# Staging the first two 512-token chunks as wholes, from tiles at the other end of SBUF

## The chip, the core and the metric

The kernel runs on one core of a Trainium2 chip. A time is the device time of one execution in microseconds (us); several executions give a median. The profiled execution is a single one, with a span (from its first instruction to its last) and a time of its own.

## What is computed

Two transformer blocks over 2048 tokens of 1024 features. Only the head of the first block matters here:

```python
mod = c_act @ w_ada + b_ada                       # 6 x 1024 numbers, from the conditioning vector c
sh1, sc1, ... = split(mod, 6)
h = rmsnorm(x, ln1_pre) * (1 + sc1) + sh1         # x: 2048 x 1024
proj = h @ w_in                                   # 22 groups of 128 columns
# then sliding-window attention over 6 of the groups, a gated recurrence over 16,
# an output projection, a mixture of experts, and a second block
```

Each matrix product is made from three products of float32r parts: every operand is split into a rounded part (`hi`) and what is left (`lo`), and `hi*lo + hi*hi + lo*hi` is summed in PSUM.

## The kernel before, in words

All generators of a stage ("lanes") are run by a scheduler, `B.run`, when the program is built. It keeps a planned clock for each engine and its own costs of operations, and lets a lane emit its next instruction when the planned clock says that its inputs are ready. So the order of the instructions on each engine is fixed by the plan, and the chip then runs each engine in that order. `Pool.get` and `B.bank` hand out buffers and wait until one is free; `B.bank("pA")` gives one of two PSUM banks of that tag, and there are four tags (`pA`, `pS`, `pU`, `pT`) of two banks, eight banks in all. Nearly every instruction is recorded at line 122, that of the helper which issues it, so the rows are told apart by their tiles.

The first stage is `P1.run`. Its lanes, around the change:

- `mod_first` loads 16 tiles of `wadaT` (128x1024 float32, 512 KB each, tiles `mh` and `ml`), seven ahead, and takes a dot product of each with the activated vector `cact` on VectorE (`mod_dot`). At the tenth it sets the flag `x`; after the sixteenth `first()` makes the scales `a1` and shifts `sh1` of the norm and sets the flag `mod`.
- `h_lane` waits for `x` and then goes over the 4 chunks of 512 tokens and the 4 tiles of 128 tokens in each: it loads a tile of `x` into one of two buffers `xl` and spawns `h_block`. That squares and sums it on ScalarE (output `jk`), takes the inverse root on VectorE (`rsqrt`, 13 small operations on tiles `xrv`, `xry`, `xrt`), scales the tile by it on GpSimd (`xl<-xl,xry`), waits for `mod`, transposes the tile in two halves of four 128x128 blocks into a bank `pT`, and gives `xl` back. For each half `h_part` evicts the four blocks with scale and shift into `hf` (one half on VectorE, one on ScalarE), rounds them on ScalarE into `hhi`, and subtracts on VectorE into `hlo`. When all eight halves of a chunk are done, `self.h[c]` is set.
- `h_tiles` gives the `hhi` and `hlo` of a chunk; there are two sets, so chunks 2 and 3 wait until chunks 0 and 1 have been used for the first half of the sequence.
- `W.lane` waits for `x`, loads the groups of `w_in`, rounds them on GpSimd (`whi`), subtracts on VectorE (`wlo`), and stores both to DRAM (`WIN`) for the second half. Four groups are held.
- `lane_a` projects: for each group, both chunks of a half (`proj`, which waits for `self.h[c]`, then 24 matmuls of 128x512 in a bank `pA`). The first group is the keys: `ev_k` evicts them into `KH` and `KL` with four ScalarE and four VectorE instructions, after the flag `("swa", half)`; the second is the values, then the queries.
- `swa(half)` opens the attention's tiles (`KH`, `KL`, `VS`, `ndist`) and runs the attention units; `hgrn` the recurrence; `mod_rest` the other 32 tiles of `wadaT`, once chunk 1 is staged.

Of the kernel before, what the change touches and what calls it, by code (L numbers as in the profile page):

```python
# [10 lines left out]
F32 = mybir.dt.float32  # L11
F32R = mybir.dt.float32r
BF16 = mybir.dt.bfloat16
# [3 lines left out]
AF = mybir.ActivationFunctionType  # L17
OP = mybir.AluOpType
# [5 lines left out]
D = 1024  # L24
KT = 8
# [3 lines left out]
BLOCK = None  # L29
# [149 lines left out]
class Pool:  # L179
    def __init__(self, pool, clock):  # L180
        self.pool, self.clock, self.rings, self.slots = pool, clock, {}, {}
# [26 lines left out]
class B:  # L208
# [15 lines left out]
        nc.vector.memset(self.eps, EPS)  # L224

    @contextmanager
    def pool(self, name):
        with self.tc.tile_pool(name=name, bufs=2, reuse_waits="tile") as p:
            yield Pool(p, self.clock)

    def phase(self, name):
# [86 lines left out]
    def run(self, *lanes, back=(), first=()):  # L318


        lanes, first = list(lanes), list(first)
        back = list(back) + [g for g in self.lanes if g not in first]
        c = self.clock
        idle = 0
        while lanes or self.spawned:
            state = BLOCK
            for g in first + self.spawned + lanes + back:
                try:
                    r = next(g)
                except StopIteration:  # L330
                    for l in (first, self.spawned, lanes, back, self.lanes):
                        if g in l:
                            l.remove(g)
                    state = 1
                    break
                if r:
                    state = r
                    break
                if r is not BLOCK:
                    state = 0  # L340
            if state:
                idle = 0
                continue
            c.now += 0.05
            idle = idle + 1 if state is BLOCK else 0
            if idle >= 400:
                assert False, "every lane is blocked"
# [28 lines left out]
            (lambda: V.scalar_tensor_tensor(out, t, 1.5, y, op0=OP.add, op1=OP.mult), (t,)))  # L376
        return out

    def rsqrt(self, ss, n, scale, name, out=None):

        V = self.nc.vector
        v, y, t = (self.small([128, n], name + z) for z in "vyt")
        out = y if out is None else out
        yi = y.bitcast(I32)
        newton = [(lambda: V.tensor_tensor(t, y, y, op=OP.mult), (y,)),
                  (lambda: V.tensor_tensor(t, t, v, op=OP.mult), (t,)),
                  (lambda: V.scalar_tensor_tensor(y, t, 1.5, y, op0=OP.add, op1=OP.mult), (t,))]
        yield from self.steps("vector",
            (lambda: V.tensor_scalar(v, ss, scale, EPS, op0=OP.mult, op1=OP.add), (ss,)),
            (lambda: V.tensor_scalar(yi, v.bitcast(I32), 1, None, op0=OP.logical_shift_right), (v,)),  # L390
            (lambda: V.tensor_scalar(yi, yi, -1.0, float(0x5F3759DF), op0=OP.mult, op1=OP.add), (y,)),
            (lambda: V.tensor_scalar(v, v, -0.5, None, op0=OP.mult), (v,)),
            *newton, *newton, *newton[:2],
            (lambda: V.scalar_tensor_tensor(out, t, 1.5, y, op0=OP.add, op1=OP.mult), (t,)))
        return out


class Weights:
# [4 lines left out]
    def __init__(self, b, ld, pool, srcs, ring, shape=(128, 1024), ahead=2, lo="vector", store=None, keep=None):  # L403
        self.b, self.ld, self.pool, self.srcs, self.ring, self.shape, self.ahead = b, ld, pool, srcs, ring, list(shape), ahead
        self.store, self.keep = store, keep or {}
        self.hl, self.eng, self.hi_eng = {}, lo, "gpsimd"
        self.extra, self.taken = None, 0
        self.writing = set()
# [105 lines left out]
def pipe(units, depth):  # L514


    live, more = [], True
    it = iter(units)
    while live or more:
        state = BLOCK  # L520
        if more and len(live) < depth:
            try:
                u = next(it)
                if u is not BLOCK:
                    live.append(u)
            except StopIteration:
                more = False
        for u in list(live):
            try:
                c = next(u)  # L530
            except StopIteration:
                state = 1
                live.remove(u)
                break
            if c:
                state = c
                break
            if c is not BLOCK:
                state = 0
        if live or more:  # L540
            yield state
# [9 lines left out]
class P1:  # L551
# [41 lines left out]
    def mod_first(self):  # L593

        b, I = self.b, self.I
        ws, n = [], 0
        for j in range(16):
            while n < min(16, j + 7):
                w = yield from self.Wp.get([128, D], F32, "m" + "hl"[n % 2], tag=("whi", "wlo")[n % 2], bufs=4)
                yield from b.load(w, I["wadaT"][n])  # L600
                ws.append(w)
                n += 1
            w = ws.pop(0)
            yield from self.mod_dot(j, w)
            b.done(w)
            if j == 9:
                self.flags.add("x")
        self.nc.vector.tensor_tensor(self.mod1, self.mod1, b.bada[:, 0:16], op=OP.add)
        self.first()
        self.flags.add("mod")  # L610
        yield 1
# [32 lines left out]
        nc.vector.tensor_scalar(self.hw, b.vec[:, HON, 0:4], 0.5, None, op0=OP.mult)  # L644


    def h_lane(self):

        b = self.b
        yield from self.wait("x")  # L650
        for c in range(4):
            for t in range(4):
                x = yield from self.ld.get([128, D], F32, "xl", bufs=self.nxl)
                r = (c * 4 + t) * 128
                yield from b.load(x, self.I["x"][r:r + 128, :])
                b.spawn(self.h_block(c, x, slice(t * 128, t * 128 + 128)))
# [405 lines left out]

    def swa(self, half):
        b, nc, I = self.b, self.nc, self.I
        with b.pool("p1a") as P:
            self.P = P
            self.la, self.lb, self.po = Lock(), Lock(), {}
            self.KH = P.tile([128, 2, 1152], F32R, name="KH", bufs=1)
            self.KL = P.tile([128, 2, 1152], F32R, name="KL", bufs=1)
            self.VS = P.tile([128, 9, 2, 2, 64], F32R, name="VS", bufs=1)  # L1070
            self.ndist = P.tile([128, 256], F32, name="ndist", bufs=1)
            nc.sync.dma_start(self.ndist, I["ndist"])
            new = [self.KH[:, :, 0:128], self.KL[:, :, 0:128], self.VS[:, 0]]
            old = [self.KH[:, :, 1024:], self.KL[:, :, 1024:], self.VS[:, 8]]
            if half:
                for a, o in zip(self.carry, new):
                    nc.gpsimd.tensor_copy(o, a.bitcast(F32))
            self.flags.add(("swa", half))
            yield from pipe(self.swa_units(half), 7)
            if half == 0:  # L1080
                for a, o in zip(self.carry, old):
                    nc.gpsimd.tensor_copy(a, o.bitcast(F32))
# [19 lines left out]
    def run(self):  # L1102
        b, tc, nc, I = self.b, self.b.tc, self.nc, self.I
        st, en = b.phase("p1")
        with st:
            b.nld, self.nxl, self.nmd = 2, 2, 1
            self.ld, self.Sp, self.X, self.POp = en("ld"), en("p1s"), en("p1x"), en("p1po")
            self.carry = [self.Sp.tile(s, F32R, name=f"c{i}", bufs=1) for i, s in enumerate(([128, 2, 128], [128, 2, 128], [128, 2, 2, 64]))]
            self.order = [4, 5, 0, 1, 2, 3], [0, 4, 5, 1, 2, 3]
            hg = [g + hd for hd in range(4) for g in (10, 6, 18, 14)]  # L1110
            once = self.order[0] + hg
            self.W = Weights(b, self.ld, self.Wp, [I["w_in"][n] for n in once] + hg + self.order[1], ring=4, shape=(128, KT, 128),
                             store=self.parts, keep={i: n for i, n in enumerate(once)})
            self.S = []
            for hd in range(4):
                s = self.Sp.tile([128, 128], F32, name=f"S{hd}", bufs=2)
                nc.vector.memset(s, 0.0)
                self.S.append(s)
            self.consts()
            b.run(self.mod_first(), self.h_tiles(), chain(self.swa(0), self.hgrn(), self.swa(1)), self.h_lane(), chain(self.wait("x"), self.W.lane()), self.lane_a(), self.mod_rest())  # L1120


NE = 32
# [1974 lines left out]
```

## Time and profile before

| what | value |
|---|---|
| median of 3 runs | 4062.14 us (4050.82 to 4066.87) |
| the profiled execution: time | 4061.26 us |
| the profiled execution: span | 4059.4 us |
| TensorE busy | 3646.1 us, 90% of the span |
| VectorE busy | 2734.8 us, 67% |
| ScalarE busy | 2283.2 us, 56% |
| GpSimd busy | 901.4 us, 22% |

A busy share is an average over stages that have different limits. Matmuls overlap in the engine, so TensorE's busy time counts some stretches of it more than once.

### The profile page before, as it was taken

To read this page: it belongs to the slowest core of one execution; us is meant where nothing else is said; L and a number is where in the kernel's file an instruction comes from. 1 tells how busy PE (TensorE), PEld (TensorE's weight loads), DVE (VectorE), ACT (ScalarE), POOL (GpSimd) and SP (SyncE) were. 2 spreads that over 40 slices of the span, in tenths; PEclk is the share of its full clock that TensorE was granted. 3 is DMA by queue.
4 is the path that set the end of the run, shared out by engine and by line. 5 is a ranking of instruction groups with operands and counts; after the bars stand their busy time and mean duration, and the time that the engine had idled before them with its cause. 6 is when DMAs were issued, how large, how long until landed. Compare 5 with 4: busy or idle time off the path is not lost.

```text
span 4059.4 us, 64576 instructions
## 1 busy us (share of the span) xinstructions
PE 3646.1 (90%) x21649; PEld 3167.4 (78%) x21649; DVE 2734.8 (67%) x7027; ACT 2283.2 (56%) x4628; POOL 901.4 (22%) x1650
## 2 busy tenths in 40 slices
PE   3999999979969999397999989999889988999997
PEld 2888788768858888296777779888678877999997
DVE  7866785697777777526366743467766656878772
ACT  3654655565546666424257755357667774676751
POOL 1310000031011100473044526111033321211110
PEclk9999999979989999598999989999889998999999
DMA  6233451125358887739887773543166527787767
GB/s 229 79 108 110 137 198 60 64 81 167 130 202 314 314 315 285 263 126 339 290 255 249 249 283 108 169 147 101 43 187 180 173 81 270 259 281 272 265 230 283
DMA packets 425744, 801.28 MB, mean 197 GB/s; under 512 B 129360, under 2 KB 245296, under 8 KB 424496
## 3 DMA queue, kind: packets, MB, share of 16 engines
q1 hardware_dynamic: 407472, 748.70, 54.3%
q0 software_dynamic: 17920, 48.26, 3.5%
q8 instruction: 176, 2.88, 0.3%
q14 instruction: 176, 1.44, 0.1%
HBM read 571.02 MB, written 234.18 MB: 198 GB/s over the span
## 4 chain that ended last, share of the span: by engine, by line
PE 37%; DMA 7%; POOL 4%; DVE 3%; issue 3%; ACT 2%; SPq 1%; POOLq 0%; DVEq 0%; ACTq 0%
PE pA L122 22%; PE pS L122 5%; PE pT L122 5%; PE pU L122 5%; POOL rot L122 1%; DMA x<-IQ 1%; SPq L122 1%; DMA x<-QB 1%; DMA tz<-TZ 1%; POOL st L122 1%; DMA Q<-QA 0%; DMA sg<-SG 0%; DVE scb L122 0%; DVE pp L122 0%; POOL QB L122 0%
## 5 line engine op out<-in xcount | busy, mean ns | idle before, releaser
L122 PE MATMUL pA<-xnl,whi 128*128 128x512 f32 x1024 | 415.3, 406 | 5.4 <-DVE st L122 5.4
L122 DVE TENSOR_TENSOR wlo<-ld,whi 128x1024 fp32r<-128x1024 f32 x271 | 328.7, 1243 | 112.6 <-ACT whi L122 74.8
L122 PE MATMUL pA<-xnh,wlo 128*128 128x512 f32 x1024 | 403.7, 394 | 0.4 <-DVE wlo L122 0.4
L122 PE MATMUL pA<-xnh,whi 128*128 128x512 f32 x1024 | 403.9, 394 | 0.0
L122 DVE TENSOR_TENSOR pp<-pT,pp 128x256 fp32r<-128x256 f32 (+1 forms) x568 | 295.1, 537 | 117.5 <-ACT pp L122 113.8
L122 ACT ACTIVATE pp<-pT 128x256 fp32r<-128x256 f32 (+1 forms) x568 | 260.6, 478 | 201.5 <-PE pT L122 189.3
L122 PE MATMUL pA<-hlo,whi 128*128 128x512 f32 x832 | 352.1, 423 | 10.0 <-issue 6.7
L122 PE MATMUL pA<-hhi,wlo 128*128 128x512 f32 x832 | 328.8, 395 | 0.0
L122 PE MATMUL pA<-hhi,whi 128*128 128x512 f32 x832 | 327.9, 394 | 0.0
L122 ACT ACTIVATE whi<-ld 128x1024 fp32r<-128x1024 f32 x212 | 213.5, 1052 | 59.0 <-PE pA L122 35.3
L122 DVE SCALAR_TENSOR_TENSOR acc<-rl,iw,acc 128x512 f32<-128x512 f32 (+3 forms) x304 | 220.8, 727 | 38.0 <-ACT rl L122 31.4
L122 PEld LDWEIGHTS pA<-xnh,wlo 128*128 128x128 f32 x1024 | 193.9, 189 | 44.8 <-DVE wlo L122 1.1
L122 ACT ACTIVATE bias<-acc,sst 128x1152 f32<-128x1152 f32 (+13 forms) x168 | 220.0, 1309 | 13.3 <-DVE sst L122 9.6
L122 PEld LDWEIGHTS pA<-xnl,whi 128*128 128x128 f32 x1024 | 195.4, 191 | 33.6 <-issue 5.8
L122 PE MATMUL pA<-wlo,xnh 128*128 128x256 f32 (+1 forms) x672 | 200.9, 299 | 22.2 <-DVE st L122 12.4
L122 PEld LDWEIGHTS pA<-xnh,whi 128*128 128x128 f32 x1024 | 194.9, 190 | 29.4
L122 PE MATMUL pU<-pp,vbS 128*128 128x256 f32 x1088 | 203.2, 301 | 10.2 <-DVE pp L122 8.3
L122 ACT ACTIVATE rl<-pS 128x512 f32<-128x512 f32 (+3 forms) x304 | 163.6, 544 | 82.4 <-PE pS L122 42.9
L122 PE MATMUL pA<-whi,xnl 128*128 128x256 f32 (+1 forms) x672 | 197.5, 294 | 4.1 <-DMA xnl<-XND 4.1
L122 PE MATMUL pA<-whi,xnh 128*128 128x256 f32 (+1 forms) x672 | 197.6, 294 | 0.0
L122 ACT ACTIVATE st<-pA 128x256 f32<-128x256 f32 (+4 forms) x160 | 73.6, 460 | 202.6 <-PE pA L122 161.5
L122 PEld LDWEIGHTS pA<-hlo,whi 128*128 128x128 f32 x832 | 159.4, 192 | 35.9 <-issue 9.4
(494 smaller groups left out, 11117.2 us busy)
## 6 DMA issues: line engine op xcount, KB each, us to landing
whi<-W2P SPq DMA_DIRECT2D x172, 512.0 KB
wlo<-W2P SPq DMA_DIRECT2D x172, 512.0 KB
ld<-in_w_gu_dram SPq DMA_DIRECT2D x128, 512.0 KB
ld<-in_w_dn_dram SPq DMA_DIRECT2D x64, 512.0 KB
W2P<-whi SPq DMA_DIRECT2D x57, 512.0 KB
W2P<-wlo SPq DMA_DIRECT2D x57, 512.0 KB
Y<-ym SPq DMA_DIRECT2D x48, 512.0 KB
xl<-in_wadaT_dram SPq DMA_DIRECT2D x32, 512.0 KB
```

The lines of the kernel that those rows point to most:

```text
L122: r = real(*a, **k)
```

## The change

`h_first(c)` takes the place of `h_lane` for chunks 0 and 1. Eight tiles of 128x1024 (`x0[c][t]`) are opened at the right end of SBUF, 32 KB of each partition. The four loads of chunk 0 are issued ahead of the `wadaT` loads, which now wait for the flag `("loads", 0)`; those of chunk 1 are issued at the flag `x`. Each chunk is squared on ScalarE into four columns of one tile; one `rsqrt` of 13 operations on 128x4 is emitted without a break (`whole=True`); the four tiles are scaled on ScalarE instead of on GpSimd. Then, for each of the 8 groups of 128 features, four transposes fill one bank, chunk 0 in all eight banks of PSUM and chunk 1 in the four of `pT` and `pU`, before `mod` is known. `h_feature` waits for `mod`, and evicts a whole bank (128x512) with scale and shift by one instruction, on VectorE or ScalarE in turn, into a half of a tile of `x0[0]`, rounds it and subtracts. `swa(0)` now waits until both chunks are staged, closes the eight tiles, and only then opens its own. `h_lane` does chunks 2 and 3 as before, after the flag `("staged", 1)`.

```diff
-    def rsqrt(self, ss, n, scale, name, out=None):
+    def rsqrt(self, ss, n, scale, name, out=None, whole=False):
...
+        if whole:
+            yield from self.on("vector", ss)
+            for f, _ in chain:
+                f()
+            yield 1
+        else:
+            yield from self.steps("vector", *chain)
         return out
...
         ws, n = [], 0
+        yield from self.wait(("loads", 0))
         for j in range(16):
...
+    def h_first(self, c):
+        b, nc = self.b, self.nc
+        if c:
+            yield from self.wait("x")
+        x = self.x0[c]
+        for t in range(4):
+            r = c * 512 + t * 128
+            yield from b.load(x[t], self.I["x"][r:r + 128, :])
+        self.flags.add(("loads", c))
+        ss = b.small([128, 4], "xss4", bufs=2)
+        for t in range(4):
+            yield from b.on("scalar", x[t])
+            jk = self.X.tile([128, D], BF16, name="jk2", bufs=1)
+            nc.scalar.activation(jk, x[t], AF.Square, accum_out=ss[:, t:t + 1])
+            yield 1
+        y = yield from b.rsqrt(ss, 4, 1.0 / D, "x4", whole=True)
+        for t in range(4):
+            yield from b.A(x[t], x[t], AF.Copy, scale=y[:, t:t + 1])
+        while c not in self.ht:
+            yield BLOCK
+        hi, lo = self.ht[c]
+        n = [0]
+        for k in range(KT):
+            pt = yield from b.bank(*(("pA", "pS", "pU", "pT") if c == 0 else ("pT", "pU")))
+            yield from b.on("tensor", pt, *x)
+            for t in range(4):
+                nc.tensor.transpose(pt[:, t * 128:t * 128 + 128], x[t][:, k * 128:k * 128 + 128], b.ident)
+            yield 1
+            b.spawn(self.h_feature(c, k, pt, hi, lo, n))
+        self.flags.add(("staged", c))
+
+    def h_feature(self, c, k, pt, hi, lo, n):
+        b = self.b
+        yield from self.wait("mod", ("staged", 0))
+        f = self.x0[0][k // 2][:, k % 2 * 512:k % 2 * 512 + 512]
+        if k % 2:
+            yield from b.A(f, pt, AF.Identity, scale=self.a1[:, k:k + 1], bias=self.sh1[:, k:k + 1])
+        else:
+            yield from b.V("tensor_scalar", f, pt, self.a1[:, k:k + 1], self.sh1[:, k:k + 1], op0=OP.mult, op1=OP.add)
+        b.done(pt)
+        yield from b.A(hi[:, k], f, AF.Copy)
+        yield from b.L(lo[:, k], f, hi[:, k])
+        n[0] += 1
+        if n[0] == KT:
+            self.h[c] = (hi, lo)
+
     def h_lane(self):
         b = self.b
-        yield from self.wait("x")
-        for c in range(4):
+        yield from self.wait(("staged", 1))
+        for c in range(2, 4):
...
     def swa(self, half):
         b, nc, I = self.b, self.nc, self.I
+        if half == 0:
+            while 0 not in self.h or 1 not in self.h:
+                yield BLOCK
+            self.xst.close()
...
+            self.xst = ExitStack()
+            xp = self.xst.enter_context(b.pool("p1xs", "right"))
+            self.x0 = [[xp.tile([128, D], F32, name=f"x0{c}{t}", bufs=1) for t in range(4)] for c in range(2)]
```

## Rows read from the trace of the kernel before

**Rows 1.** Busy time by stretch (stretch, length, busy us and instructions of each engine):

```profile
core 0: us, PE busy (x) PEld busy (x) DVE busy (x) ACT busy (x) POOL busy (x), PEclk, DMA share, GB/s
0.00:36.00 36.00, 0.00 (x0) 0.00 (x0) 28.06 (x69) 4.73 (x7) 3.02 (x6) 1.00 0.86 328
36.00:65.00 29.00, 9.85 (x41) 8.04 (x42) 24.73 (x84) 14.89 (x32) 8.87 (x8) 1.00 0.81 271
65.00:88.00 23.00, 10.79 (x50) 8.49 (x49) 18.50 (x70) 16.32 (x34) 3.54 (x3) 0.76 0.28 93
88.00:820.00 732.00, 710.66 (x4103) 597.58 (x4103) 512.46 (x1439) 392.74 (x859) 76.41 (x122) 0.98 0.31 107
820.00:920.00 100.00, 72.88 (x368) 60.61 (x367) 86.24 (x309) 57.05 (x168) 38.44 (x69) 0.78 0.33 100
```

**Rows 2.** What TensorE waited for, 0 to 88 us:

```profile
PE pT L122 <- POOL xl L122: 57.9, 6, 36.3
PE pT L122 <- ACT jk L122: 7.0, 1, 7.0
PE pA L122 <- DVE hlo L122: 2.5, 1, 2.5
```

**Rows 3.** TensorE in order of time (start us, length us, idle before):

```profile
36.31 1.97 PE L122 MATMUL pT<-ident,xl 128*128 128x128 f32 x8 [36.31 <-POOL xl L122]
...
64.72 0.78 PE L122 MATMUL pA<-hlo,whi 128*128 128x512 f32 x1
...
68.59 1.04 PE L122 MATMUL pT<-ident,xl 128*128 128x128 f32 x8
...
83.20 1.97 PE L122 MATMUL pT<-ident,xl 128*128 128x128 f32 x8 [6.96 <-ACT jk L122]
87.66 0.79 PE L122 MATMUL pA<-hlo,whi 128*128 128x512 f32 x1 [2.49 <-DVE hlo L122]
...
101.14 0.47 PE L122 MATMUL pA<-hlo,whi 128*128 128x512 f32 x1 [0.85 <-DVE KL L122]
```

**Rows 4.** VectorE and ScalarE in order of time, the dots and one inverse root:

```profile
8.51 1.23 DVE L122 CUSTOM_DVE_ANT_0 jk<-mh,cact 128x1024 bf16<-128x1024 f32 x1
...
12.64 1.23 DVE L122 CUSTOM_DVE_ANT_0 jk<-ml,cact 128x1024 bf16<-128x1024 f32 x1 [0.35 <-DMA ml<-in_wadaT_dram]
...
29.25 0.17 DVE L122 TENSOR_TENSOR mod<-mod,bada 128x16 f32<-128x16 f32 x1
29.46 0.17 DVE L122 SCALAR_TENSOR_TENSOR a<-mod,vec 128x8 f32<-128x8 f32 x1
...
89.56 0.15 DVE L122 TENSOR_SCALAR xrv<-xss 128x1 f32<-128x1 f32 x1 [0.95 <-ACT jk L122]
...
91.75 0.16 DVE L122 SCALAR_TENSOR_TENSOR xry<-xrt,xry 128x1 f32<-128x1 f32 x1
```

**Rows 5.** Busy time by stretch again, the two with only loads and dots:

```profile
10.00:20.00 10.00, 0.00 (x0) 0.00 (x0) 9.38 (x15) 0.00 (x0) 0.00 (x0) 1.00 1.03 414
20.00:30.00 10.00, 0.00 (x0) 0.00 (x0) 9.34 (x20) 0.26 (x2) 0.00 (x0) 1.00 1.03 409
```

**Rows 6.** Groups by tile and shape, 0 to 100 us (busy us, mean ns, idle before):

```profile
L122 DVE TENSOR_TENSOR hlo<-hf,hhi 128x512 fp32r<-128x512 f32 x16 | 13.5, 851 | 2.1 <-ACT hhi L122 2.0
L122 ACT ACTIVATE hf<-pT,mod,a 128x128 f32<-128x128 f32 x32 | 12.6, 452 | 15.4 <-PE pT L122 13.3 <-DVE xry L122 2.0
L122 DVE TENSOR_SCALAR hf<-pT,a,mod 128x128 f32<-128x128 f32 x32 | 12.2, 403 | 1.5 <-PE pT L122 1.5
L122 ACT ACTIVATE jk<-xl 128x1024 bf16<-128x1024 f32 x10 | 10.5, 1053 | 4.5 <-DMA xl<-in_x_dram 4.5
L122 ACT ACTIVATE hhi<-hf 128x512 fp32r<-128x512 f32 x16 | 9.8, 625 | 3.0 <-DVE hf L122 2.8
L122 DVE TENSOR_TENSOR wlo<-ld,whi 128x1024 fp32r<-128x1024 f32 x5 | 6.1, 1219 | 3.9 <-POOL whi L122 3.9
L122 DVE TENSOR_TENSOR KL<-pA,KH 64x512 fp32r<-64x512 f32 x7 | 4.8, 686 | 2.0 <-ACT KH L122 2.0
L122 ACT ACTIVATION_READ_ACCUMULATOR jk<-xl 128x1 f32 x10 | 1.9, 187 | 0.0
L122 ACT ACTIVATE cact<-cb 128x1024 f32<-128x1024 f32 x1 | 1.1, 1056 | 3.4 <-DMA cb<-in_c_dram 3.4
```

**Rows 7.** Instructions that read or write `hf` and `hlo` (ns min/median/max):

```profile
L122 ACT ACTIVATE hf<-pA x20: 597/599/607, 100.3 to 787.2; 128x512 f32<-128x512 f32 x20
...
L122 DVE TENSOR_TENSOR hlo<-hf,hhi x32: 677/686/1498, 41.0 to 487.0; 128x512 fp32r<-128x512 f32 x32
```

**Rows 8.** The keys of chunk 1 leave PSUM, in order of time:

```profile
94.89 1.20 ACT L122 ACTIVATE KH<-pA 64x512 fp32r<-64x512 f32 x2 [5.35 <-PE pA L122]
...
99.59 1.40 DVE L122 TENSOR_TENSOR KL<-pA,KH 64x512 fp32r<-64x512 f32 x2 [1.27 <-ACT KH L122]
```

**Rows 9.** VectorE and GpSimd side by side, in order of time:

```profile
31.85 1.04 POOL L122 TENSOR_SCALAR whi<-ld 128x1024 fp32r<-128x1024 f32 x1 [31.41 <-DMA ld<-in_w_in_dram]
31.97 0.93 DVE L122 SCALAR_TENSOR_TENSOR xry<-xrt,xry 128x1 f32<-128x1 f32 x1
...
34.05 1.23 DVE L122 TENSOR_TENSOR wlo<-ld,whi 128x1024 fp32r<-128x1024 f32 x1
34.22 2.04 POOL L122 TENSOR_SCALAR xl<-xl,xry 128x1024 f32<-128x1024 f32 x1 [1.33 <-DVE xrt L122]
```

More of the change, by code (lines that the diff above doesn't have):

```diff
@@ L226, in pool @@
     @contextmanager
-    def pool(self, name):
-        with self.tc.tile_pool(name=name, bufs=2, reuse_waits="tile") as p:
+    def pool(self, name, side=None):
+        with self.tc.tile_pool(name=name, bufs=2, side=side, reuse_waits="tile") as p:
             yield Pool(p, self.clock)
@@ L387, in rsqrt @@
                   (lambda: V.scalar_tensor_tensor(y, t, 1.5, y, op0=OP.add, op1=OP.mult), (t,))]
-        yield from self.steps("vector",
+        chain = (
             (lambda: V.tensor_scalar(v, ss, scale, EPS, op0=OP.mult, op1=OP.add), (ss,)),
@@ L1118, in run @@
                 self.S.append(s)
+            self.xst = ExitStack()
+            xp = self.xst.enter_context(b.pool("p1xs", "right"))
+            self.x0 = [[xp.tile([128, D], F32, name=f"x0{c}{t}", bufs=1) for t in range(4)] for c in range(2)]
             self.consts()
-            b.run(self.mod_first(), self.h_tiles(), chain(self.swa(0), self.hgrn(), self.swa(1)), self.h_lane(), chain(self.wait("x"), self.W.lane()), self.lane_a(), self.mod_rest())
+            b.run(self.mod_first(), self.h_tiles(), chain(self.swa(0), self.hgrn(), self.swa(1)), self.h_first(0), self.h_first(1), self.h_lane(), chain(self.wait("x"), self.W.lane()), self.lane_a(), self.mod_rest())
 NE = 32
```

## The prediction

> **What bounds the kernel now.** I read the table of busy time by stretch first. From 88 to 820 us TensorE is busy 710.66 of 732 us at a granted clock of 0.98, above every other engine; ahead of that it does almost nothing: no instruction up to 36 us, 9.85 us of work in the next 29, 10.79 in the next 23 [rows 1]. So the first stage has two parts: 88 us of preparation, in which TensorE starves, and a long run in which it is the limit. The waits say on what it starves: 57.9 us for the tiles of x that GpSimd scales, 7.0 for a square, 2.5 for the last `hlo` [rows 2]. In order of time, the first projection (keys, chunk 0) starts at 64.72 us, and the second (keys, chunk 1) only at 87.66; from there the run is dense [rows 3]. The start of the keys of chunk 1 is therefore the point to follow: everything behind it is a chain of TensorE work, and whatever moves this point moves the end, as long as no later work starts at a time of its own.
>
> **The start: loads and dots.** Before, loads and dots keep each other's pace: DMA moves 414 and 409 GB/s [rows 5], so a tile of 524,288 bytes takes 1.27 us, and sixteen dots run from 8.51 to 29.25 us, 20.7 us [rows 4]. The fourth big tile after the constants has landed at 12.6 us (its dot waited until then) [rows 4]. Now the first four tiles are those of x, so the last of them lands at about 12.6, and `wadaT` follows from 13.9 (12.6 + 1.27). Four squares on ScalarE at 1.05 + 0.19 us [rows 6] keep up with the loads; the last ends at 13.9. One inverse root takes 2.35 us (89.56 to 91.91, 13 operations) [rows 4], and I take the same for 128x4. It sits on VectorE either before the dots or between them; either way VectorE has 2.35 + 20.7 us to do from 13.9, so the sum is 36.9, and the scales are there at 37.3 (0.4 behind, as before), against 29.6: the change first *loses* 7.6 us.
>
> **Chunk 0.** Scaling moves to ScalarE: four copies of 128x1024, bounded by the row of that shape at 1.06 us [rows 6], from 16.2 to 20.5. The 32 transposes cost between 1.04 and 1.97 us for eight [rows 3]; I take the slow row, since TensorE has idled: 7.9 us, done at 28.4. Both are free: they have 8.9 us of cover before the scales at 37.3. Without the cover they would cost up to 12.2 us.
>
> Then eight features: four evictions on each engine, eight roundings on ScalarE, eight subtractions on VectorE. No row has the eviction of 128x512 with scale and shift. For ScalarE it lies between 0.60 us (an eviction of that shape) [rows 7] and four pieces of 0.45, 1.8 [rows 6]; I take 0.60, since it is one instruction. For VectorE between 0.40 (a quarter of it) and 1.6 (four quarters); I take 0.69, that of another PSUM read of 512 columns [rows 6]. With 0.63 for a rounding [rows 6] and 0.69 for a subtraction [rows 7], ScalarE has 4 x 0.60 + 8 x 0.63 = 7.4 us and VectorE 4 x 0.69 + 8 x 0.69 = 8.3. Before, a chunk cost ScalarE 16 x 0.45 + 8 x 0.63 = 12.2, VectorE 16 x 0.40 + 8 x 0.69 = 11.9 and 52 small operations of four roots besides, where now there are 13.
>
> **Chunk 1.** Its loads stand on SP's queue behind the last `wadaT` load, which waits until the eighth dot gives its buffer back (13.9 + 2.35 + 8 x 1.3 = 26.6 us); the DMA queue is full until then, so they land behind it, from 34.2 to 38.0. The weights' loads and their stores are queued behind them, first weights at about 39.3; the keys' weights are needed only at 47, the others later. ScalarE from 37.3: four squares 5.0, chunk 0's features 7.4 (under which the root's 2.35 on VectorE hide), four copies 4.2: 53.9. The first bank is transposed by 54.9 (0.5 to 1.0 us), eight features follow at VectorE's pace, 8.3, and the last one's chain of 0.60 + 0.63 + 0.69 is still to run: **65.1 us** for the keys of chunk 1, against 87.66. Bounds: ScalarE's bare sum, 37.3 + 5.0 + 7.4 + 4.2 + 7.4 = 61.3; and 72, if chunk 1's transposes run slow and in the way (7.9 in place of 4.2) and ScalarE stands some 3 us. So 22.6 us are won at this point, 16 to 26 by the bounds. VectorE's own sum (8.3 + 2.35 + four `wlo` of 1.22 + 8.3 from 37.3 = 61.1) does not overtake it.
>
> A row on TensorE's clock: the eight transposes behind 6.96 us of idling took 1.97 us, those between projections 1.04 [rows 3], the granted clock of that stretch being 0.76 [rows 1]. The Trainium skill, *TensorE: Matmul & The Clock Gate*, "What's actually happening", says that the slow state (1.2 GHz) is the default and activity lifts it to 2.4; that speaks against staging in two bursts with nothing between. By the rule chunk 1's transposes are slow too; by the faster row they are not: 68.8 against 65.1 if none of it is hidden.
>
> A row on VectorE: a small operation took 0.93 us while GpSimd rounded a weight, and GpSimd's scaling took 2.04 beside a subtraction [rows 9]; the mean `hlo` here was 0.85 us [rows 6], the median over the kernel 0.69 [rows 7]. *SBUF — State Buffer* of the Trainium skill, "Who interferes with whom", has the two engines share a port pair that one holds for a whole instruction. Taking the scaling off GpSimd removes eight such holders; by the mean `hlo` chunk 1 would end 1.3 us later, by the median as above.
>
> **The new wait.** `swa(0)` opens `KH` only when both chunks are staged, so chunk 0's keys, projected from about 47 us, hold one of two `pA` banks until 65. Behind them on TensorE stand chunk 1's keys (other bank) and then the values, which need the first bank. An eviction of keys takes 6.1 us (94.89 to 100.99) [rows 8], a projection with its slow start about as long, so the values wait 0 to 6 us; I take 1. `ndist` is loaded later, but needed much later.
>
> **Sum.** 22.6 - 1 = 21.6 us; the profiled execution's 4061.3 becomes 4039.7. The median of the runs shown lies 0.9 above it, so I say 4040.
>
> **Rivals.**
> 1. *The point moves, but less.* VectorE and ScalarE hold their planned order, the plan's costs are not the chip's, and one head-of-line wait of 5 to 10 us in this burst puts the keys at 68 to 80: 4044 to 4056. For it: ScalarE stands on VectorE and TensorE 15.4 us in the old staging [rows 6]. Against: fewer, longer instructions.
> 2. *The change does not do what it says*: the long run is not bound by TensorE, and the head start is eaten later: 4058 to 4064. For it: weight loads fill only 82% of that run (597.58 of 732 us). *Trainium Kernel Development and Optimization* in the Trainium skill, "Performance Expectations", calls matmul busy time a bad measure because matmuls overlap. Against: nothing in this stage starts by the clock on the wall; VectorE (512.46) has more room still [rows 1].
> 3. *More than planned*: squares before 37 us, transposes warm, and later order no worse: keys at 58 (4033) and a seam, further on, that idles less.
> 4. *Slower.* The planner writes the order of everything behind the change anew. The place is the seam at 820 to 920 us, where TensorE idles 27 us at a clock of 0.78 while VectorE is busy 86 [rows 1]. A second gap of that size, 27 us, would eat the gain (4045); it ends slower by half a per cent only from 42 us of new idling on: 4083.
>
> **How the numbers follow.** Half a per cent, 20.3 us, is about what a measurement of this kernel can tell from no change; the line is at 4041.8, near my forecast. The forecast's own case (keys at 61 to 68, 4036 to 4044) gets 0.50, 0.37 of it faster and 0.13 the same; rival 1 0.24, same; rival 2 0.06, same; rival 3 0.14, faster; rival 4 0.06, of which 0.05 slower and 0.01 the same. Faster 0.51, same 0.44, slower 0.05. The range, 4023 to 4059, leaves out rival 2's upper part, rival 4 and the tail of 3.
>
> **What the next profile would show.** Scales ready at 36 to 38 us; 32 transposes of chunk 0 done before; first projection near 47; second at 61 to 68, and 101.14 [rows 3] (values of chunk 1) some 20 us earlier; the seam at about 800 to 900 with idling near 27. I am wrong if the second projection starts past 72, if TensorE waits on `KL` for more than 6 us, or if the distance from that projection to the end is not the 3972 us of before within 8 us.

## The result, and the profile after

The changed kernel takes 4101.36 us (median of 4 runs, 4097.64 to 4104.14), the kernel before 4059.81 us beside it: a ratio of 1.0103 [1.008, 1.0126]. It is slower by 1%, where 4040 was forecast. The profiled execution has a span of 4098.2 us and a time of 4099.96 us.

First the stretches of [rows 1], after the change:

```profile
core 0: us, PE busy (x) PEld busy (x) DVE busy (x) ACT busy (x) POOL busy (x), PEclk, DMA share, GB/s
0.00:36.00 36.00, 6.19 (x32) 5.08 (x32) 23.54 (x52) 11.20 (x14) 0.20 (x4) 0.93 0.94 354
36.00:65.00 29.00, 11.25 (x48) 9.06 (x49) 23.29 (x46) 22.39 (x36) 5.11 (x4) 0.56 0.80 280
65.00:88.00 23.00, 19.93 (x77) 15.78 (x76) 13.32 (x41) 8.77 (x18) 3.26 (x3) 0.85 0.32 108
88.00:820.00 732.00, 707.35 (x4110) 594.10 (x4110) 517.40 (x1459) 400.18 (x880) 77.73 (x128) 0.99 0.30 105
820.00:920.00 100.00, 73.87 (x350) 61.21 (x350) 80.44 (x285) 54.60 (x155) 37.49 (x63) 0.76 0.38 119
```

From 65 to 88 us TensorE now has 19.93 us of work where it had 10.79, and the seam at 820 to 920 idles as before. Nothing here tells of a loss. TensorE's waits up to 88 us say what it starves on now, beside [rows 2]:

```profile
PE pT L122 <- ACT x L122: 28.0, 4, 26.3
PE pA L122 <- ACT x L122: 19.5, 4, 17.8
PE pA L122 <- DVE KL L122: 3.1, 1, 3.1
```

GpSimd's scaling is gone from the list; the two big waits are those for the first copies of chunk 0 and of chunk 1, ahead of which TensorE has nothing to do. The third is new here, and I put it down to the hold of `swa(0)`. TensorE in order of time, beside [rows 3]:

```profile
17.84 0.47 PE L122 MATMUL pA<-ident,x 128*128 128x128 f32 x1 [17.84 <-ACT x L122]
...
24.69 1.04 PE L122 MATMUL pT<-ident,x 128*128 128x128 f32 x8
52.01 0.47 PE L122 MATMUL pT<-ident,x 128*128 128x128 f32 x1 [26.28 <-ACT x L122]
...
57.27 0.78 PE L122 MATMUL pA<-hlo,whi 128*128 128x512 f32 x1
...
62.11 0.47 PE L122 MATMUL pA<-hlo,whi 128*128 128x512 f32 x1
...
67.00 0.39 PE L122 MATMUL pA<-hlo,whi 128*128 128x512 f32 x1
...
75.67 0.76 PE L122 MATMUL pA<-hlo,whi 128*128 128x512 f32 x1 [3.07 <-DVE KL L122]
76.23 0.63 PE L122 MATMUL pA<-hhi,whi 128*128 128x512 f32 x1
...
99.44 0.22 PE L122 MATMUL pS<-KH,Q 128*128 128x128 f32 x1
```

The first projection has 24 matmuls: three from 57.27, the other 21 from 62.11 at 0.23 us each. The next, at 67.00, is the second projection (keys of chunk 1), which stood at 87.66: **20.7 us won**, 22.6 forecast. At 75.67 the values of chunk 0 wait 3.07 us for `KL`. The first scores of the attention (`pS<-KH,Q`) start at 99.44; in the trace of before they start at 116.49:

```profile
116.49 0.22 PE L122 MATMUL pS<-KH,Q 128*128 128x128 f32 x1
```

So 17.1 us of lead are left there. The other engines in the same stretch of the changed kernel, beside [rows 4, 9]:

```profile
14.25 0.17 DVE L122 TENSOR_SCALAR x4v<-xss 128x4 f32<-128x4 f32 x1 [5.79 <-ACT jk L122]
...
16.64 4.27 ACT L122 ACTIVATE x<-x,x4y 128x1024 f32<-128x1024 f32 x4 [2.42 <-DVE x4y L122]
...
36.99 0.17 DVE L122 SCALAR_TENSOR_TENSOR a<-mod,vec 128x8 f32<-128x8 f32 x1
...
37.49 0.78 ACT L122 ACTIVATE x<-pA,mod,a 128x512 f32<-128x512 f32 x1
...
37.92 0.81 DVE L122 TENSOR_SCALAR x<-pS,a,mod 128x512 f32<-128x512 f32 x1
...
41.26 1.98 POOL L122 TENSOR_SCALAR whi<-ld 128x1024 fp32r<-128x1024 f32 x1 [0.18 <-DMA ld<-in_w_in_dram]
...
42.26 1.52 DVE L122 TENSOR_TENSOR hlo<-x,hhi 128x512 fp32r<-128x512 f32 x1
...
49.13 1.04 POOL L122 TENSOR_SCALAR whi<-ld 128x1024 fp32r<-128x1024 f32 x1 [1.88 <-DVE x4t L122]
49.17 1.01 DVE L122 SCALAR_TENSOR_TENSOR x4y<-x4t,x4y 128x4 f32<-128x4 f32 x1
...
50.80 4.27 ACT L122 ACTIVATE x<-x,x4y 128x1024 f32<-128x1024 f32 x4 [2.23 <-DVE x4y L122]
...
56.37 1.28 DVE L122 TENSOR_TENSOR hlo<-x,hhi 128x512 fp32r<-128x512 f32 x2
...
69.12 0.68 DVE L122 TENSOR_TENSOR hlo<-x,hhi 128x512 fp32r<-128x512 f32 x1
```

The two at 56.37 are the last subtractions of chunk 0, the one at 69.12 is the last of chunk 1.

So the first scores come earlier, as was meant. To find where the time went I cut both traces at three marks that each kernel passes once: `ROW`, stored by the first block, is read back into `crow` (the second block starts), `xnh` is loaded, and the first `yt` is loaded (the tail starts). Busy time between them, of the kernel before:

```profile
0.00:1643.00 1643.00, 1485.14 (x7951) 1234.18 (x7951) 1229.71 (x2992) 913.31 (x1795) 201.59 (x279) 0.96 0.49 174
1643.00:2406.00 763.00, 644.70 (x3631) 558.99 (x3632) 432.68 (x1078) 386.62 (x894) 329.16 (x583) 0.91 0.77 256
2406.00:3355.00 949.00, 866.34 (x5131) 752.71 (x5129) 570.70 (x1660) 590.58 (x1284) 266.97 (x634) 0.95 0.45 140
3355.00:4059.00 704.00, 649.89 (x4938) 621.54 (x4938) 501.73 (x1297) 392.70 (x656) 103.68 (x154) 0.96 0.77 267
```

and of the changed kernel:

```profile
0.00:1632.00 1632.00, 1489.72 (x7951) 1236.70 (x7951) 1210.21 (x2889) 916.38 (x1781) 195.73 (x272) 0.95 0.50 175
1632.00:2392.00 760.00, 645.69 (x3629) 559.67 (x3630) 430.74 (x1077) 378.92 (x871) 326.57 (x583) 0.91 0.78 258
2392.00:3380.00 988.00, 889.60 (x5133) 770.19 (x5131) 571.35 (x1661) 601.30 (x1307) 263.59 (x634) 0.93 0.43 134
3380.00:4098.00 718.00, 654.44 (x4938) 624.82 (x4938) 501.54 (x1297) 392.24 (x656) 103.03 (x154) 0.96 0.75 261
```

The reader should compare the second column, the length, where the counts of matmuls (in brackets) say that it is the same work. Up to the second block 11 us are won, and 3 more up to `xnh`. Then the same 5,131 matmuls (and two more) take 988 us instead of 949, and the last 4,938 take 718 instead of 704: 53 us are lost more than 2,300 us behind the last instruction that the change touches.

### The profile page after: what moved, and what is told of

Its sections match the earlier page's. It is cut to its first block, busy times and chain, and to the rows that moved or that the text cites. A ratio compares the mean times of both kernels' runs of the same rounds, so it can differ in the third digit from the quotient of the medians.

```text
span 4098.2 us, 64411 instructions
## 1 busy us (share of the span) xinstructions
PE 3679.4 (90%) x21649; PEld 3191.4 (78%) x21649; DVE 2713.8 (66%) x6924; ACT 2288.8 (56%) x4614; POOL 888.9 (22%) x1643
## 5 line engine op out<-in xcount | busy, mean ns | idle before, releaser
L122 ACT ACTIVATE bias<-acc,sst 128x384 f32<-128x384 f32 (+13 forms) x168 | 220.1, 1310 | 11.0 <-DVE sst L122 7.1
L122 PE MATMUL pU<-pp,vbS 128*128 128x256 f32 x1088 | 207.3, 303 | 20.9 <-DVE pp L122 16.2
L122 PE MATMUL pS<-kbS,qd 128*128 128x512 f32 (+3 forms) x640 | 179.3, 386 | 12.6 <-DVE bst L122 11.8
```

The lines of the kernel that those rows point to most:

```text
L122: r = real(*a, **k)
```

## The cause, read from the order of the instructions

From the second block on each engine has the same number of instructions in both kernels (the bracketed counts of the last three rows add up alike, 13,700 for TensorE); what differs is their order. That order comes from the scheduler, whose lanes emit an instruction when this holds (its clock `now` goes on in steps):

```python
t = max(c.now, c.t[eng])
if c.t[eng] <= c.now + LOOK[eng] and all(c.at(a) <= t + slack for a in aps):
    return
...
c.now += 0.05
```

The change shortens the plan of the first stage, so at the start of the second block's stage (`S3.run`) the planned state has moved: TensorE's planned clock from 2060.9489 to 2053.3367, every other engine's by the same 7.6122, but `now` from 1079.05 to 1071.45, by 7.60, since it moves in steps of 0.05. These are numbers of the plan, not times on the chip. The gap between the two clocks was 981.898907 and is now 981.886740: a difference of 0.0122, a quarter of a step. With the gap changed, each comparison above falls a little earlier or later, and some fall the other way: early in the norm stage of the second block transposes of `cx` and of `st` change places on TensorE, the later instructions follow, and in the two traces only the last 578 of TensorE's 21,649 matmuls stand again as before.

That can be tested without touching anything else: one line at the start of `S3.run` sets `now` so that the gap is the one or the other. With the gap of before, the changed kernel has the second block of before, instruction for instruction, on every engine; so nothing else that the planner sees there decides its order.

## The experiments

**The new staging with the order of before (e1).**

```diff
     def run(self):                       # S3, the second block
...
+        self.b.clock.now = self.b.clock.t["tensor"] - 981.8989071115107
         order = []
```

> The changed kernel, with the planner's notion of now, at the start of the second block, set as far behind the engines' planned clocks as it stands in the kernel before (0.012 us less than in the changed kernel). From there on every engine has the order of instructions of the kernel before. Theory 1 (the loss is the order that the planner wrote for the second block, and nothing else): the 12.6 us won up to the end of the first block stay, about 4047 us, and the second block takes as long as before. Theory 2 (the loss is an effect of the new staging itself on the later stages, through SBUF places, the clock or DMA): about 4101, as the changed kernel.

Measured: 4054.82 us, median of 10 runs, against 4064.23 of the kernel before on the same chip; ratio 0.9976 [0.9962, 0.999]. So the staging with this order makes the kernel faster, by 9.4 us; theory 1 holds, with a little less than its 12.6. In a second set of runs of the same kernel:

> The new staging with the old second-block order once more, to tell a gain of a few tenths of a per cent from none. Theory 1: 8 to 13 us below the kernel before on the same chip. Rival (the first look was chance, and the second block gives the lead back in its transfers): no difference beyond 3 us.

Measured: 4056.57 us against 4065.73, ratio 0.9982 [0.997, 0.9994], 9.2 us. Of the kernels timed in several runs this is the fastest, ahead of the kernel before and of the changed one.

**The old staging with the order of after (e2).** The same line, with 981.886740, in the kernel before.

> The kernel before, with the same number set to that of the changed kernel: old staging, and in the second block the order of the changed kernel. Theory 1: it loses what the changed kernel lost behind the first block, 51 us, and ends at about 4111. Theory 2: about 4060, no change.

Measured: 4116.31 us, ratio 1.0129 [1.0106, 1.0153]. The kernel before, with none of the change in it, becomes 52 us slower by the order of the second block alone. The stretches between the marks, of e1 and then of e2:

```profile
0.00:1630.00 1630.00, 1487.62 (x7951) 1234.28 (x7951) 1209.42 (x2889) 917.08 (x1781) 194.98 (x272) 0.96 0.50 175
1630.00:2397.00 767.00, 647.59 (x3630) 560.73 (x3631) 435.06 (x1078) 387.13 (x894) 326.41 (x583) 0.91 0.77 255
2397.00:3351.00 954.00, 870.52 (x5132) 755.95 (x5130) 571.56 (x1660) 590.93 (x1284) 268.12 (x634) 0.95 0.44 139
3351.00:4056.00 705.00, 649.99 (x4938) 621.00 (x4938) 502.05 (x1297) 392.80 (x656) 103.84 (x154) 0.96 0.77 266
```

```profile
0.00:1644.00 1644.00, 1485.97 (x7951) 1234.87 (x7951) 1228.90 (x2992) 913.18 (x1795) 202.82 (x279) 0.96 0.50 173
1644.00:2403.00 759.00, 640.30 (x3629) 556.72 (x3630) 431.27 (x1077) 377.65 (x871) 326.65 (x583) 0.92 0.78 259
2403.00:3394.00 991.00, 890.88 (x5133) 771.72 (x5131) 571.38 (x1661) 602.21 (x1307) 263.99 (x634) 0.93 0.43 133
3394.00:4110.00 716.00, 648.91 (x4938) 618.47 (x4938) 501.23 (x1297) 392.42 (x656) 103.11 (x154) 0.97 0.76 262
```

With the two kernels above this is a table of four. The first stretch goes by the staging: 1643 and 1644 with the old, 1632 and 1630 with the new. The third and fourth go by the order: 949 + 704 and 954 + 705 with the old, 988 + 718 and 991 + 716 with the new. The second stretch also goes by the order, the other way: 763 and 767 with the old, 760 and 759 with the new. Staging and order hardly touch each other.

What the worse order costs is seen between e1 and the changed kernel, which have the same staging. TensorE's waits from the `xnh` load to the end, the rows that differ most, of e1:

```profile
PE pT L122 <- DMA x<-QB: 31.8, 10, 26.2
PE pA L122 <- DVE tz L122: 12.3, 8, 2.5
PE pU L122 <- DVE pp L122: 8.6, 15, 1.6
...
PE pS L122 <- DVE bst L122: 7.2, 11, 2.8
...
PE pT L122 <- DVE pp L122: 4.3, 3, 3.1
```

and of the changed kernel:

```profile
PE pT L122 <- DMA x<-QB: 35.8, 8, 31.1
PE pA L122 <- DVE tz L122: 16.6, 9, 3.5
PE pU L122 <- DVE pp L122: 16.2, 26, 1.8
PE pS L122 <- DVE bst L122: 12.2, 19, 3.0
PE pT L122 <- DVE pp L122: 8.4, 7, 2.2
```

All rows of these two lists add up to 125.7 and 148.8 us: 23 us more of waiting. Four are for the load `x<-QB`; most of the rest lies in many short pieces (0.6 to 1.8 us on average in the other rows shown). Half of it is for `pp`, which VectorE reads out of PSUM right ahead of the matmul that needs it. The other half of the loss is no wait: TensorE's busy time for the same matmuls rises by 19.1 us in the third stretch (870.52 to 889.60) and by 4.5 in the fourth, at a granted clock of 0.93 instead of 0.95 in the third. (This busy time counts each moment once, other than the section on the time before says: the 24 matmuls from 67.00 add up to 9.4 us and fill 5.6.) The records of the granted clock have two levels, 1.2 and 2.4 GHz. TensorE's busy time at the lower one grows from 62.7 to 93.6 us in the third stretch and from 24.9 to 32.1 in the fourth. A row of matmuls at the lower level stands 0.43 us apart instead of 0.23, so about half of that growth, some 19 of the 23.6 us, is put down to the clock; this is an estimate from these figures. Together waits and busy time are 47 us, which is what the two stretches are longer (954 + 705 to 988 + 718).

**Other phases (e3, e4, f4, g1, g2).** If 0.0122 of the plan decides, other small shifts should move the time too, in either direction. The same line, with the gap smaller than that of after by 0.0125 (e3) and 0.025 (e4), and larger than that of before by 0.0125 (f4 in the kernel before, g1 in the changed one) and 0.025 (g2 in the changed one).

> The changed kernel with that number moved 0.0125 us the other way: a third order for the second block, the first block untouched. Theory 1: the span up to the second block is that of the changed kernel within 2 us, and the end lies elsewhere, anywhere from 4040 to 4110, as the order falls. Theory 2: 4101 within 5.

> The same with 0.025 us: a fourth order. Theory 1: again another end between 4040 and 4110; theory 2: 4101 within 5.

> The kernel before, with the planner's now moved back by 0.0125 us at the start of the second block, nothing else. Theory 1 (any such shift writes another order, and the kernel before stands on a good one): first block as before within 2 us, the end elsewhere, between 4050 and 4110, likely later than 4062. Theory 2 (only the changed staging is sensitive): 4062 within 5.

> The new staging with the second-block order of f4_before_shift (the kernel before with the planner's now moved back by 0.0125 us), which ended at 4093 there. Theory 1 (staging and order add up): about 12 us less than that kernel, 4078 to 4084, and still later than the kernel before. Rival (the gain of the staging shows only with the one order): 4093 or later.

> The new staging with one more order, the planner's now moved back by 0.025 us from where the kernel before has it. Theory 1: an end of its own between 4040 and 4110, with the first block as in the changed kernel; by the five orders seen so far (4055, 4073 to 4078 and three at 4093 and above, for either staging) an end above 4060 is likelier than one below.

Measured, with the ratio to the kernel before on the same chip:

| gap | old staging | new staging |
|---|---|---|
| 981.861740 | | e4: 4077.60, 1.0031 [1.0016, 1.0046] |
| 981.874240 | | e3: 4102.72, 1.0079 [1.0049, 1.0108] |
| 981.886740 (of after) | e2: 4116.31, 1.0129 [1.0106, 1.0153] | after: 4101.36, 1.0103 [1.008, 1.0126] |
| 981.898907 (of before) | before: 4059.81 | e1: 4054.82, 0.9976 [0.9962, 0.999] |
| 981.911407 | f4: 4092.98, 1.0056 [1.0038, 1.0074] | g1: 4087.73, 1.0051 [1.0033, 1.0069] |
| 981.923907 | | g2: 4102.73, 1.0086 [1.0065, 1.0107] |

e3 alone fits both of its theories, since 4102.72 is also within 5 us of 4101; e4 and f4 fit only the first, and g2 came out above 4060 as the likelier case. e3's second block starts at 1636.2, where 1631.5 within 2 us was expected: the seven profiles that have the new staging and the same first block spread over 6.7 us at this mark (1629.5 to 1636.2). The kernel before took 4059.81 to 4069.54 in the four sets, so the ratios compare better than the times.

Six orders, with the new staging, spread over 48 us, and that of before is the best of them; none of the other five is within 20 us of it. In rows two and three of the new staging the orders are different and the time is the same. f4 and g1 have one order and differ by 5 us only (2 by the ratio), with intervals of the ratio that overlap; g1 fell between its two forecasts. There the head start is not seen in the time, and whether it is lost to that order or to the spread of few runs (6 and 5) is open.

**What each part of the staging is worth.** These three keep the order of before in the second block (the line of e1, left out of the cuts below), so that the head can be read. Their first blocks have orders of their own. Chunk 0 staged as a whole, chunk 1 by the old `h_lane` (f3, one run):

```diff
-        yield from self.wait(("staged", 1))
-        for c in range(2, 4):
+        yield from self.wait(("staged", 0))
+        for c in range(1, 4):
...
-                        for t in range(4)] for c in range(2)]
+                        for t in range(4)] for c in range(1)]
...
-            b.run(..., self.h_first(0), self.h_first(1), self.h_lane(), ...)
+            b.run(..., self.h_first(0), self.h_lane(), ...)
```

> Half of the change: only chunk 0 as a whole, chunk 1 tile by tile as before; old order in the second block. Before, chunk 1's keys started 22.9 us behind chunk 0's. Theory A (each chunk gives its own share): chunk 0 staged at about 50, keys of chunk 1 at 71 to 75, so chunk 1's part of the change is worth 5 to 8 of the 20.8 us. Theory B (most of the gain is that both go through as wholes): keys of chunk 1 at 78 or later.

Measured: 4065.38 us. The keys of chunk 1, in TensorE's order of time of f3:

```profile
49.82 1.97 PE L122 MATMUL pT<-ident,xl 128*128 128x128 f32 x8 [3.48 <-POOL xl L122]
...
73.69 0.80 PE L122 MATMUL pA<-hlo,whi 128*128 128x512 f32 x1 [4.62 <-DVE hlo L122]
```

At 73.69 they are 14 us ahead of before, against 20.7 with both chunks whole; the first scores start at 107.41, 9 ahead against 17. Chunk 0 as a whole is worth some 9 us, chunk 1 some 8 more. GpSimd's scaling is waited for again (49.82). The keys came where theory A had them, 71 to 75. At the start of the second block (1640.5 us) only 2 of the 9 us are left against the trace of before (1642.6), in this one profile.

Chunk 0's loads behind those of `wadaT`, as before (f2, one run), so that the scales come early and the staging has no cover:

```diff
-        yield from self.wait(("loads", 0))
...
-        if c:
-            yield from self.wait("x")
+        yield from self.wait("x")
```

> The changed kernel with the old order in the second block, and with the loads of chunk 0 behind those of wadaT, as before the change. Theory A (putting them ahead costs its 7.5 us, since the scales come later): scales back at 29.6, keys of chunk 1 at 60 to 63 in place of 66.9, scores 4 to 7 us earlier. Theory B (the squares, copies and transposes of chunk 0, 9.2 us on ScalarE and 8 on TensorE, lose their cover and cost as much): keys of chunk 1 at 65 to 69.

Measured: 4053.82 us. The scales are there at 30.4, 6.8 us earlier, but the keys of chunk 1 start at 67.89, later than the changed kernel's 67.00 and in theory B's range. The values of chunk 0, in TensorE's order of time of f2, start 3.2 us later:

```profile
78.86 0.63 PE L122 MATMUL pA<-hlo,whi 128*128 128x512 f32 x1 [3.43 <-DVE KL L122]
```

and the first scores at 102.40 against 99.44. Loading x first delays the scales by 7 us and hides the staging of chunk 0: a gain of 3 us at the scores, 2 to 4 against the seven profiles with the first block of after, whose scores start at 98.35 to 100.40. It is the small part of the change; most of the 17 us comes from whole tiles and whole banks. Farther on the 3 us are not seen: the second block of f2 starts at 1633.1, within the range of those seven, and its one time is no longer than e1's.

The hold of `swa(0)` (f1): `h_lane` stays out of the way until chunk 1's keys are evicted, to see whether the wait at 75.67 comes from chunk 2's work on VectorE and ScalarE.

```diff
-        yield from self.wait(("staged", 1))
+        yield from self.wait(("staged", 1), ("k", 0, 1))
```

> The changed kernel with the old order in the second block, and with the staging of chunk 2 held until the keys of chunk 1 have left PSUM. In the changed kernel the values of chunk 0 waited 3.1 us for the keys' eviction and then ran 14 matmuls at the slow clock; the first attention scores began at 99.4 us. Theory A (the squares and small root operations of chunk 2, which stand between the evictions on ScalarE and VectorE, make the wait): scores begin at 95 to 97. Theory B (the wait for both chunks makes it: two evictions of keys must run one behind the other): 99 within 1. The whole: 4050 to 4056.

Measured: the wait is 2.18 us instead of 3.07 and the scores start at 98.71. In the seven profiles with the first block of after, the waits for `KL` up to the scores add up to 3.0 to 6.1 us. So f1 waits less than all of them, by 0.8 to 3.9 us, but its scores are not earlier than theirs (98.35 to 100.40): theory B, and what chunk 2's work costs at the scores is too little to be seen. The whole kernel takes 4072.60 us, ratio 1.0015 [1.0001, 1.0028] where e1 had 0.9976 and 4050 to 4056 were expected. This edit lets the planner write the *first* block anew: the second block, in the order of before, starts at 1646.5 (`crow<-ROW`), 15 us behind the changed kernel, although the scores had started earlier than there. The new order of the first block is the likely cause; the later staging of chunk 2 itself was not told apart from it. A kernel without the hold was not tried, so that the hold itself makes the rest of the wait is argued and not shown.

## Why the prediction was wrong

The step that failed is in its first paragraph: everything behind the second projection "is a chain of TensorE work, and whatever moves this point moves the end, as long as no later work starts at a time of its own". The last line of the prediction gave the test, a distance of 3972 us from that projection to the end, within 8. It is 4098.2 - 67.0 = 4031 us. Two things stand in its place. The larger is the new order of the second block, 47 to 52 us (e1, e2). The smaller is that the chain does not carry the whole lead even with the order held: the distance is 3991 us in e1 and 3982 in e1b, and 9.3 us of the lead reach the end. The planner's rewriting was seen, as rival 4, but with the wrong place, the wrong price and too small a chance (0.06). I looked for it where TensorE already idles, in the seam [rows 1], and that seam is unchanged (73.87 us busy against 72.88). The loss lies in the second block, which no row of the prediction shows, in stretches where nothing stood out: 53 us, above the 42 us from which that rival decides. Its 4045 was also added up wrongly: 27 us more on top of 4040 are 4067. What no trace of before can tell is whether a new order is good or bad; that one would be written could be read from the scheduler, since an edit ahead moves the planned clocks.

The steps of the working, one by one:

- **Scales at 37.3:** at 37.2 (36.99 + 0.17). **Root 2.35:** from 14.25 to 16.60, ahead of the dots. **Copies to 20.5:** to 20.9. **Transposes of chunk 0 done at 28.4:** at 25.7, as each tile's first transpose follows its copy. Right.
- **Feature costs:** a bank's eviction with scale and shift takes 0.78 us on ScalarE, not 0.60, and 0.81 on VectorE, not 0.69. Four of each make 0.7 and 0.5 us a chunk.
- **First projection at 47:** three matmuls at 57.27, the rest from 62.11. Its place on TensorE is behind three banks (twelve) of chunk 1's transposes, and the other five banks stand in the midst of it. Its data is late too: VectorE ends the last `hlo` of chunk 0 at 57.65, where the working had 37.3 + 8.3 = 45.6, since chunk 1's root and four `wlo` stand among the eight in its order.
- **Second projection at 65.1 (61 to 72):** at 67.0; over the seven profiles with this first block the mean is 65.8, over the three with the old one 88.6, so 22.8 us are won. The number is right, the way to it is not, and that is luck. The working starts the projection at the end of chunk 1's last `hlo`. That end is 69.80, 4.7 us later; the projection starts ahead of it, as it takes the features one by one, and what holds it is its place behind the first projection on TensorE.
- **Transposes of chunk 1 warm or slow:** slow. From 52 to 62 us the granted clock is 0.53, nearly all at 1.2 GHz, and eight transposes take up to 1.91 us, behind 26.28 us of idling. *TensorE: Matmul & The Clock Gate* of the Trainium skill, "What's actually happening", says that slow is the default and activity lifts it. The trace agrees: from 65 to 88 us, with TensorE busy for 19.93 of 23 us, the granted clock is 0.85. At 75.67, after 3.07 us of waiting, fourteen matmuls again stand 0.43 us apart instead of 0.23.
- **The new wait, 1 us (0 to 6):** 3.07 us, and 14 x 0.20 = 2.8 for the slow matmuls behind it: 5.9, the upper end. In the seven profiles with this order the waits for `KL` are 3.0 to 6.1 us in all, and six to fourteen matmuls behind them are slow. The working left out the slow matmuls.
- **VectorE beside GpSimd:** at 49.17 a small operation of the root takes 1.01 us instead of 0.16 while GpSimd rounds a weight from 49.13 to 50.17, as in [rows 9]. *SBUF — State Buffer* of the Trainium skill, "Who interferes with whom", has the two engines hold a shared port pair in turn. The trace agrees: VectorE loses 0.85 us there, and as much at 42.26, where a subtraction takes 1.52 us instead of 0.68 beside a rounding that takes 1.98 instead of 1.04.
- **The net gain, 21.6:** even with the order held it is 9.3 us. Of the 20.7 won at the second projection, 17.1 are left at the first scores. At the start of the second block the seven profiles with the new staging and the first block of after stand at 1629.5 to 1636.2, the three with the old at 1642.6 to 1644.1: 10.4 us between their means. From there to the end hardly more is lost. By the means of the same profiles the lead is 22.8 us at the second projection, 18.5 at the first scores (99.15 against 117.63) and 10.4 at the second block. What is lost between the scores and the second block was not traced to a cause; the first block's order differs too, and that was not held fixed.

## What to carry to other kernels

Where a planner writes the order when the kernel is built, an edit has two effects: the one that was meant, and a new order of everything that is planned behind it, which here was worth five times as much (47 to 52 us against 9). Compare such kernels with the order behind the edit held fixed, or over several phases of the plan, before a verdict on the edit itself; and when the order of before is a lucky one, pin it. A head start at the beginning is not a gain at the end: count it at marks along the way.

## What was not expected

- 0.0122 of planned time, with every instruction the same, moved the kernel by 52 us (4064.23 to 4116.31), 1.3%; of six orders tried, the one of before was the fastest by 20 us or more.
- A worse order costs twice: 23 us in waits, mostly short ones, and as much again in busy time for the same matmuls, most of it by a lower granted clock (0.95 to 0.93 from the `xnh` load to the tail).
- Which of the reordered instructions of the second block cost the most is open: the list of waits names `pp`, `bst`, `tz` and the load `x<-QB`, but no run put one of them back alone.
